# A two-layer hybrid trunk: ten of the 22 tiles of the third FFN by seven products, all hyena filters beside the first FFN, the modulations spread anew, one pool of five PSUM banks

## The chip, the cores and the metric

The kernel runs on one core of a Trainium2 chip. The metric is the time of one execution on the device in microseconds (us); lower is better. TensorE (PE in the profile) multiplies matrices, VectorE (DVE) and ScalarE (ACT) work elementwise, GpSimd (POOL) takes a few small operations, SyncE (SP) issues the DMAs. Each engine works through its own instructions in the order of the program and waits on semaphores.

## The reference

Two layers act on 640 tokens of width 1024: 128 context tokens and 512 latent tokens. Each layer is an FFN, a group of four token mixers, and a second FFN, each behind a normalization that is scaled and shifted by a modulation of the layer:

```python
mod = (jax.nn.silu(cond) @ lp['w_mod'] + lp['b_mod'])[:, None, :]
sh1, sc1, g1, sh2, sc2, g2, sh3, sc3, g3 = jnp.split(mod, N_MOD, axis=-1)
x = x + 0.5 * g1 * swiglu(modulate(rmsnorm(x, nw[0]), sh1, sc1), lp['ffn_w_in'][0], lp['ffn_w_out'][0])
y, s_ssd, s_ret, k, v = token_mixing(modulate(rmsnorm(x, nw[1]), sh2, sc2), lp, ssd_s0, ret_s0, ctx_kv)
x = x + g2 * y
x = x + 0.5 * g3 * swiglu(modulate(rmsnorm(x, nw[2]), sh3, sc3), lp['ffn_w_in'][1], lp['ffn_w_out'][1])

def swiglu(h, w_in, w_out):
    gate, up = jnp.split(h @ w_in, 2, axis=-1)
    return (jax.nn.silu(gate) * up) @ w_out
```

The inner width of an FFN is 2816, 22 tiles of 128. One of the mixers is hyena: a long convolution whose kernels ("filters") come from a small network with sines that depends on the weights alone, not on the tokens.

## The kernel before

The work on the tokens is a chain of stages, with `x` kept transposed in SBUF as 8 tiles of 128 features by 640 tokens, in two halves g = 0 and 1 of 320 columns: FFN1, mixers and FFN2 of layer 0, then FFN3, mixers and FFN4 of layer 1. A scheduler orders the instructions of each engine when the program is built; at run time the order is fixed.

**Products.** Every fp32 operand is split into a high and a low part (`hi`, `lo` of a weight; `hh`, `hl` of the normalized x; `gh`, `gl` of the gated product). The high part is a ScalarE cast, the low part a VectorE subtraction (`split`, `wsplit`). A product is then three matmuls (`mm3`): hi by hh, hi by hl, lo by hh. TensorE can't take the third one before VectorE has written `lo`.

**FFN1 and FFN3** use `ffn`: 22 direct tiles, each with a gate and an up weight of 1024 columns, 2 weights x 2 halves x 8 x 3 = 96 matmuls. The shift of the modulation rides as two more columns in half 0 (322 columns). After each chunk of tiles (5, 5, 5, 4, 3) a down pass multiplies by the output weights and adds into `x` (`accumulate`, the `x<-mm,gate,x` rows).

**FFN2 and FFN4** use `ffn7`: two direct tiles (320 columns), then 20 "quads". A quad computes the 2x2 block product of one tile's gate and up weights with the two halves by seven products instead of eight: 7 x 4 x 3 = 84 matmuls. VectorE adds weight blocks into `sa` and `sb` and splits them; the sums of the token blocks (`nv<-nv`, split into `th` and `tl`) are formed once at the start of the stage, by `sums`, behind each of the first two direct tiles. The first product of a quad goes into a PSUM tile `mb`, the second into `mm`, the third (`T3`, which needs `sa`) into `mc`. `norm7` is the normalization that leaves the sums' raw material behind; `norm` is that of `ffn`.

**Modulations.** Except for a few at the start, each 128-row tile of `w_mod` is loaded by DMA (`wm`) and reduced on VectorE against the broadcast condition, once for each of two conditions (`wmj<-wm,condb`, a "piece", pinned in the order of the program), then a small addition writes `mod`. A generator yields piece by piece; `ffn` and `ffn7` take them at a rate (RATES) per half-tile, per column of a down pass or per quad, from a list (`todo`) for each FFN.

**Filters.** The filters of layer 0 stand beside FFN1, those of layer 1 beside FFN3: small matmuls, sines, and DMAs to DRAM.

Of the kernel before, what the change touches and what calls it, by code (L numbers as in the profile page):

```python
# [19 lines left out]
EPS = 1e-6  # L20
NEG = -1.0e30
GCOLS = ((0, 128, 0), (128, 320, 1)), ((0, 320, 1),)
FFN_CHUNKS = (5, 5, 5, 4, 3), (4, 4, 4, 4, 3, 3)
KMAIN = 19


# [27 lines left out]
class Trunk:  # L54
# [38 lines left out]
        self.nc.tensor.transpose(out, in_, self.ident[b : b + n, b : b + n])  # L93

    def mx(self, *shape):

        self.turn = (self.turn + 1) % 5
        if self.wide and self.turn >= 3:
            t = self.xtp.tile([128, 512], F32, tag="xt", name="mx")
        else:  # L100
            t = self.mxp.tile([128, 512], F32, tag="mx", name="mx")
        return self.shaped(t, shape)

    @staticmethod
# [23 lines left out]
    def setup(self):  # L128
        tc, nc, ctx, I = self.tc, self.nc, self.ctx, self.I
        pool = lambda name, bufs=1, **k: ctx.enter_context(tc.tile_pool(name=name, bufs=bufs, **k))  # L130
        self.cp = cp = pool("const")
        self.sp = pool("small", 2)
        self.wp = pool("w", 3)
        self.ringp = pool("ring", NB)
        self.mmp = pool("mmp", 3, space=PSUM)
        self.xtp = pool("xtp", 2, space=PSUM)
        self.mxp = pool("mxp", 3, space=PSUM)
        self.turn, self.wide = 0, True
        self.ssum, self.V = {}, {}
# [283 lines left out]
    def ffn(self, li, w, todo, rate, after_group, ahead=()):  # L423
        I, n = self.I, 2 * w
        ff = 0
        with self.tc.tile_pool(name="ffn", bufs=2, side="right", reuse_waits="tile") as mp, self.tmp(), \
                self.tc.tile_pool(name="mods", bufs=1, side="right", reuse_waits="tile") as modp:
            mods = self.modulation(todo, modp, bufs=MBUF, pin=PIN) if todo else iter(())
            credit = 0.0
            for ci, nk in enumerate(FFN_CHUNKS[0]):  # L430
                G = []
                for f in range(ff, ff + nk):
                    wg, wu = (ahead[i] if 2 * f + i < len(ahead) else self.wload(I["ffnin"][li, w, 2 * f + i], 1024)
# [22 lines left out]
                            next(mods, None)  # L456
                            credit -= 1.0
                    G.append([(gh[:, 320 * g : 320 * g + 320], gl[:, 320 * g : 320 * g + 320]) for g in range(2)])
                if ci == len(FFN_CHUNKS[0]) - 1:
                    for _ in mods:  # L460
                        pass
                if ci < len(FFN_CHUNKS[0]) - 1:
                    for m in range(8):
                        hi, lo = self.wload(I["ffnoutA"][li, w, m, :, ff * 128 : (ff + nk) * 128], nk * 128)
                        for g in range(2):
# [27 lines left out]
    def quad(self, li, w, f, sp, mp, halves):  # L493
# [12 lines left out]
        add(sa[:, 1], sb[:, 0], a11, SUB)  # L506
        add(sb[:, 1], a12, sa[:, 1], SUB)
        new = lambda pool, tag, name: pool.tile([128, 512], F32, tag=tag, name=name)[:, :320]
        A, B, C = new(self.mmp, "mm", "mm"), new(self.xtp, "xt", "mb"), new(self.xtp, "xt", "mc")
        sg = mp.tile([128, 640], F32, tag="sg", name="sg", bufs=2)  # L510

        def copied(ps, name):
# [32 lines left out]
        self.split(gh[:, o:], gl[:, o:], sg[:, o:])  # L545
        self.G.append([(gh[:, 320 * g : 320 * g + 320], gl[:, 320 * g : 320 * g + 320]) for g in range(2)])

    def ffn7(self, li, w, todo, rate, after_group):
        I, n = self.I, 2 * w
        pool = lambda name: self.tc.tile_pool(name=name, bufs=2, side="right", reuse_waits="tile")  # L550
        with pool("ws") as sp, pool("ffn") as mp, pool("mods") as modp, self.tmp():
            self.wide = False
            mods = self.modulation(todo, modp, bufs=MBUF, pin=PIN) if todo else iter(())
            credit = 0.0
            self.G = []

            def finish(q):
                for _ in q:
# [2 lines left out]
            def down(ff, nk):  # L561

                G, self.G = self.G[:nk], self.G[nk:]
                for m in range(8):
                    hi, lo = self.wload(I["ffnoutA"][li, w, m, :, ff * 128 : (ff + nk) * 128], nk * 128)
                    for g in range(2):
                        ps = self.mmp.tile([128, 512], F32, tag="mm", name="mm")[:, :320]
                        self.mm3(ps, [(hi[:, k * 128 : (k + 1) * 128], lo[:, k * 128 : (k + 1) * 128]) + G[k][g]
                                      for k in range(nk)])
                        self.accumulate(li, n, m, g, ps)  # L570
                    next(mods, None)

            def direct(f):

# [4 lines left out]
                for g in range(2):  # L579
                    c = slice(320 * g, 320 * g + 320)  # L580
                    self.act(sg[:, c], self.unit(ws[0], g, shifts=False), AF.Silu)
                    self.tt(sg[:, c], self.unit(ws[1], g, shifts=False), sg[:, c], MUL)
                    self.split(gh[:, c], gl[:, c], sg[:, c])
                self.G.append([(gh[:, 320 * g : 320 * g + 320], gl[:, 320 * g : 320 * g + 320]) for g in range(2)])

            for f in range(NDIR):
                direct(f)
                if f < 2:
                    self.sums(f)
            for j in range(2):  # L590
                self.split(self.hw[0][1][:, 2 * j : 2 * j + 2, 0:320], self.hw[1][1][:, 2 * j : 2 * j + 2, 0:320], self.V[0][j])
            ends = [sum(FFN_CHUNKS[1][: i + 1]) for i in range(len(FFN_CHUNKS[1]))]
            prev = None
            for f in range(NDIR, 22):
                q = self.quad(li, w, f, sp, mp, f == 21)
                next(q)
                if prev is not None:
                    next(prev)
                next(q)
                if prev is not None:  # L600
                    finish(prev)
                    if f in ends:
                        ci = ends.index(f)
                        down(f - FFN_CHUNKS[1][ci], FFN_CHUNKS[1][ci])
                prev = q
                credit += rate
                while credit >= 1.0:
                    next(mods, None)
                    credit -= 1.0
            finish(prev)  # L610
            for _ in mods:
                pass
            nk = FFN_CHUNKS[1][-1]
            ws = [self.wload(I["ffnoutB"][li, w, b], 1024) for b in range(3)]
            G = self.G
            for g in range(2):
                for m in range(8):
# [7 lines left out]
                                      ws[b][1][:, j * 128 : (j + 1) * 128]) + G[k][g])  # L625
                    self.mm3(ps, parts)
                    self.accumulate(li, n, m, g, ps)
                    if li + 1 < NL:
                        self.square(m, g)
                if g:  # L630
                    next(done, None)
                done = after_group(g)
                next(done, None)
            next(done, None)
            self.wide = True


    def sin(self, pool, a, ps, b, fr):
# [684 lines left out]

    def mixers(self, li, kern):
        I = self.I
        if FPOS[li] == 2:
            kern.update(self.filters([li]))
        hy = [[self.conv_unit(li, 2 * j + h, PC.hy_cw, PC.hy_cb, 2 * j + h, False) for h in range(2)] for j in range(3)]
        if FPOS[li] == 3:
            kern.update(self.filters([li]))  # L1330
        YH = self.hyena(li, hy, *kern[li])
        Y = list(YH)
        for name in ORDER:
# [83 lines left out]
    def run(self):  # L1417
        self.setup()
        with self.tc.tile_pool(name="start", bufs=2, side="right", reuse_waits="tile") as p, self.tmp():
# [16 lines left out]
            ahead = [self.wload(self.I["ffnin"][0, 0, i], 1024) for i in range(2)]  # L1436
            for n in norms:
                next(n, None)
        kern = self.filters([0]) if FPOS[0] == 0 else {}
        todo = [[(0, i) for i in range(2, 9)] + [(1, 0)], [(1, 1)],  # L1440
                [(1, i) for i in range(2, 9)], []]
        for li in range(NL):
            def n1(g):
                if g == 0:
# [47 lines left out]
EACT = 1
# [164 lines left out]
```

## Time and profile before

| | |
|---|---|
| median of 3 runs | 2803.92 us (2802.38 to 2805.83) |
| profiled execution | 2796.57 us |
| its span in the profile | 2794.8 us |
| mean granted TensorE clock | 0.987 of full speed |
| PE, DVE, ACT busy | 97%, 69%, 36% |
| DMA | 300.52 MB, mean 108 GB/s |

The profile shows one execution. Busy shares are averages over stages that have different limits; which engine is waited for is read from single stretches. In this kernel the FFNs lie at about 56 to 563 us, 985 to 1410, 1437 to 1932 and 2354 to 2795, the mixers at 565 to 960 and 1946 to 2332, with short transitions between them.

### The profile page before, as it was taken

Reading aid. Unit: us, or ns where it says so; the run is one execution under the profiler, and the core shown is the slowest. Engines: PE = TensorE matmul, PEld = TensorE weight load, DVE = VectorE, ACT = ScalarE, POOL = GpSimd, SP = SyncE. Lnnn points to the kernel's source line nnn. Section 1 sums busy time; section 2 is a strip of 40 time slices with the busy share of each in tenths; the row PEclk is TensorE's granted clock in tenths of the full one; section 3 lists DMA queues with packets and bytes.
Section 4 is the critical chain, followed back from the end, with each engine's and each line's share of the span. In section 5 each row is a group of like instructions: output and inputs, shape, how many; then the busy total and the mean of one; then the engine's idle time right before and its main releaser. Section 6 shows DMA issues by size and latency. Waiting matters only on the chain.

```text
span 2794.8 us, 45752 instructions
## 1 busy us (share of the span) xinstructions
PE 2708.9 (97%) x17990; PEld 2601.4 (93%) x17990; DVE 1921.8 (69%) x4040; ACT 1001.2 (36%) x2047; POOL 115.6 (4%) x191
## 2 busy tenths in 40 slices
PE   5999999999999999999999999999999999999999
PEld 3899999999889899999989999998999888999999
DVE  5867677666765688766677676676568467766666
ACT  3222222332544353333442223223336434334432
POOL 0000000100010200000020000002001002000000
PEclk9999999999999999999999999999999999999999
DMA  7454544421213123222235444443213021222222
GB/s 265 145 183 144 159 143 162 136 81 63 80 51 99 52 76 117 85 86 76 82 138 181 146 144 137 143 155 99 80 57 101 18 72 59 83 81 72 83 73 94
DMA packets 121169, 300.52 MB, mean 108 GB/s; under 512 B 20062, under 2 KB 44974, under 8 KB 120572
## 3 DMA queue, kind: packets, MB, share of 16 engines
q1 hardware_dynamic: 120956, 297.61, 33.1%
q8 instruction: 142, 2.33, 0.3%
q14 instruction: 71, 0.58, 0.1%
HBM read 283.36 MB, written 14.20 MB: 106 GB/s over the span
## 4 chain that ended last, share of the span: by engine, by line
PE 89%; DVE 5%; POOL 1%; issue 1%; ACT 1%; DMA 1%; SPq 0%; POOLq 0%; ACTq 0%; DVEq 0%
PE mm L88 70%; PE mx L88 10%; PE mc L88 5%; PE mb L88 3%; PE mx L93 2%; DVE lo L61 1%; DVE x L70 1%; POOL nsum L294 1%; ACT hi L76 0%; DMA E<-cumd 0%; DVE wmj L278 0%; DVE hl L61 0%; DVE nx L70 0%; DVE gl L61 0%; POOL nrs L125 0%
## 5 line engine op out<-in xcount | busy, mean ns | idle before, releaser
L88 PE MATMUL mm<-hh,hi 128*128 128x320 f32 (+2 forms) x3136 | 993.0, 317 | 9.1 <-ACT hh L76 4.0
L88 PE MATMUL mm<-hh,lo 128*128 128x320 f32 (+2 forms) x3136 | 989.5, 316 | 7.7 <-DVE lo L61 7.7
L88 PE MATMUL mm<-hl,hi 128*128 128x320 f32 (+2 forms) x3136 | 990.4, 316 | 2.1 <-DVE hl L61 2.1
L76 ACT CAST hi<-raw 128x1024 fp32r<-128x1024 f32 (+4 forms) x406 | 346.0, 852 | 858.1 <-PE mm L88 809.4
L88 PEld LDWEIGHTS mm<-hh,hi 128*128 128x128 f32 (+1 forms) x3136 | 596.6, 190 | 19.3 <-ACT hh L76 5.6
L88 PEld LDWEIGHTS mm<-hh,lo 128*128 128x128 f32 (+1 forms) x3136 | 598.9, 191 | 16.0 <-DVE lo L61 8.4
L88 PEld LDWEIGHTS mm<-hl,hi 128*128 128x128 f32 (+1 forms) x3136 | 597.1, 190 | 13.5 <-issue 5.6
L61 DVE TENSOR_TENSOR lo<-raw,hi 128x1024 fp32r<-128x1024 f32 (+4 forms) x406 | 395.5, 974 | 183.0 <-ACT hi L76 182.0
L88 PE MATMUL mm<-gh,hi 128*128 128x320 f32 x1408 | 437.5, 311 | 7.2 <-DVE x L70 6.7
L88 PE MATMUL mm<-gl,hi 128*128 128x320 f32 x1408 | 435.2, 309 | 1.8 <-DVE gl L61 1.4
L88 PE MATMUL mm<-gh,lo 128*128 128x320 f32 x1408 | 434.5, 309 | 0.0
L70 DVE SCALAR_TENSOR_TENSOR x<-mm,gate,x 128x128 f32<-128x128 f32 (+2 forms) x624 | 253.8, 434 | 181.1 <-PE mm L88 178.6
L278 DVE CUSTOM_DVE_ANT_0 wmj<-wm,condb 128x1024 bf16<-128x1024 f32 x264 | 321.2, 1217 | 2.4 <-ACT condb L73 1.2
L88 PEld LDWEIGHTS mm<-gh,hi 128*128 128x128 f32 x1408 | 264.3, 188 | 13.6 <-PE mm L88 9.7
L88 PEld LDWEIGHTS mm<-gl,hi 128*128 128x128 f32 x1408 | 264.4, 188 | 5.8 <-DVE gl L61 4.4
L88 PEld LDWEIGHTS mm<-gh,lo 128*128 128x128 f32 x1408 | 264.5, 188 | 0.0
L70 DVE SCALAR_TENSOR_TENSOR gu<-mm,cg,sg 128x128 f32<-128x128 f32 x132 | 54.2, 436 | 157.7 <-ACT cg L76 103.6
L294 POOL TENSOR_TENSOR nsum<-nsum,nsq 128x320 f32<-128x320 f32 x60 | 54.2, 904 | 1384.3 <-ACT nsq L73 946.6
L88 PE MATMUL mc<-th,lo 128*128 128x320 f32 x320 | 98.7, 309 | 0.1
L88 PE MATMUL mc<-th,hi 128*128 128x320 f32 x320 | 98.7, 308 | 0.0
L88 PE MATMUL mc<-tl,hi 128*128 128x320 f32 x320 | 98.6, 308 | 0.0
L76 ACT COPY cg<-mm 128x2 f32<-128x2 f32 x88 | 14.1, 160 | 213.6 <-PE mm L88 213.2
(283 smaller groups left out, 3247.6 us busy)
## 6 DMA issues: line engine op xcount, KB each, us to landing
raw<-in_ffnin SPq DMA_DIRECT2D x176, 512.0 KB, 3.5
wm<-in_wmodT SPq DMA_DIRECT2D x132, 512.0 KB, 3.6
raw<-in_mixin SPq DMA_DIRECT2D x52, 512.0 KB, 3.4
raw<-in_ffnoutA SPq DMA_DIRECT2D x80, 256.0 KB, 2.6
raw<-in_ffnoutA SPq DMA_DIRECT2D x48, 320.0 KB, 2.8
wms<-in_wmod SPq DMA_DIRECT2D x12, 512.0 KB, 3.4
raw<-in_ffnoutB SPq DMA_DIRECT2D x12, 512.0 KB, 3.4
raw<-in_mixout SPq DMA_DIRECT2D x16, 384.0 KB, 3.0
```

The source lines that it names most:

```text
L61: self.nc.vector.tensor_tensor(out, a, b, op=op)
L70: self.nc.vector.scalar_tensor_tensor(out, a, s, b, op0=op0, op1=op1)
L76: self.nc.scalar.copy(out, in_)
L88: return self.nc.tensor.matmul(out, lhsT=lhsT, rhs=rhs, start=start, stop=stop, **k)
L93: self.nc.tensor.transpose(out, in_, self.ident[b : b + n, b : b + n])
L278: return self.nc.vector.tensor_tensor_reduce(junk, raw, cb, 1.0, 0.0, op0=MUL, op1=ADD, accum_out=out)
L294: (adder or (self.nc.vector if g and m > 5 else self.nc.gpsimd)).tensor_tensor(s, s, sq, op=ADD)
```

## The change

- FFN3 moves from `ffn` to `ffn7`, with 12 direct tiles and 10 quads; FFN2 and FFN4 keep 2 and 20. The transition into FFN3 therefore uses `norm7`.
- All FFNs use the chunks 5, 5, 5, 4, 3; `ffn7` now runs down passes among the direct tiles too.
- The filters of both layers are computed beside FFN1.
- The modulations are divided among the FFNs in another way, FFN4 gets some, and `ffn7` takes them at three rates: per direct half-tile, per column of a down pass, per quad.
- The two PSUM pools of 2 and 3 banks become one of 5.

```diff
-FFN_CHUNKS = (5, 5, 5, 4, 3), (4, 4, 4, 4, 3, 3)
+FFN_CHUNKS = 5, 5, 5, 4, 3
...
-        self.turn = (self.turn + 1) % 5
-        if self.wide and self.turn >= 3:
-            t = self.xtp.tile([128, 512], F32, tag="xt", name="mx")
-        else:
-            t = self.mxp.tile([128, 512], F32, tag="mx", name="mx")
+        t = self.mxp.tile([128, 512], F32, tag="mx", name="mx")
...
-        self.xtp = pool("xtp", 2, space=PSUM)
-        self.mxp = pool("mxp", 3, space=PSUM)
-        self.turn, self.wide = 0, True
+        self.mxp = pool("mxp", 5, space=PSUM)
...
-        A, B, C = new(self.mmp, "mm", "mm"), new(self.xtp, "xt", "mb"), new(self.xtp, "xt", "mc")
+        A, B, C = new(self.mmp, "mm", "mm"), new(self.mxp, "mx", "mb"), new(self.mxp, "mx", "mc")
...
-    def ffn7(self, li, w, todo, rate, after_group):
+    def ffn7(self, li, w, todo, ndir, rates, after_group):
...
-            credit = 0.0
             self.G = []
+            credit = [0.0]
+
+            def some(rate):
+
+                credit[0] += rate
+                while credit[0] >= 1.0:
+                    next(mods, None)
+                    credit[0] -= 1.0
...
-                    next(mods, None)
+                    some(rates[1])
...
                     self.split(gh[:, c], gl[:, c], sg[:, c])
+                    some(rates[0])
...
-            for f in range(NDIR):
+            ends = [sum(FFN_CHUNKS[: i + 1]) for i in range(len(FFN_CHUNKS))]
+            for f in range(ndir):
                 direct(f)
                 if f < 2:
                     self.sums(f)
+                if f + 1 in ends:
+                    nk = FFN_CHUNKS[ends.index(f + 1)]
+                    down(f + 1 - nk, nk)
...
                 prev = q
-                credit += rate
-                while credit >= 1.0:
-                    next(mods, None)
-                    credit -= 1.0
+                some(rates[2])
...
-        kern = self.filters([0]) if FPOS[0] == 0 else {}
-        todo = [[(0, i) for i in range(2, 9)] + [(1, 0)], [(1, 1)],
-                [(1, i) for i in range(2, 9)], []]
+        kern = self.filters(range(NL))
+        todo = [[(0, i) for i in range(2, 9)], [(1, 0), (1, 1)],
+                [(1, i) for i in range(2, 8)], [(1, 8)]]
...
-                    if g == 0:
-                        self.shifts(li + 1, 0)
-                    yield from self.norm(li + 1, 0, g)
+                    yield from self.norm7(li + 1, 0, g)
...
-            self.ffn(li, 0, todo[2 * li], RATES[2 * li], n1, () if li else ahead)
+            if li == 0:
+                self.ffn(li, 0, todo[0], RATES[0], n1, ahead)
+            else:
+                self.ffn7(li, 0, todo[2], NDIR[1], RATES[2], n1)
+                self.fac.close()
...
-            self.ffn7(li, 1, todo[2 * li + 1], RATES[2 * li + 1], n3)
-            self.fac.close()
+            self.ffn7(li, 1, todo[2 * li + 1], NDIR[2 * li], RATES[2 * li + 1], n3)
+        self.fac.close()
...
-NDIR = 2
+NDIR = 2, 12, 2
...
-RATES = 2.3, 1.0, 1.9, 1.0
+RATES = 2.0, (1.5, 1.0, 0.5), (2.2, 1.0, 1.0), (2.0, 1.0, 3.0)
```

**How it moves instructions.** VectorE before, in the second direct tile of FFN2 and the first quad, up to the split of that quad's first sum (`lo<-sa`); the split of the quad's gate weights, `lo<-raw` 128x1024, stands five rows ahead of these, and the first modulation piece of the stage comes eleven rows behind them:

```order
L61 TENSOR_TENSOR tl<-nv,th 128x2x320
L61 TENSOR_TENSOR gl<-sg,gh 128x320
L61 TENSOR_TENSOR nv<-nv 128x640
L61 TENSOR_TENSOR sb<-raw 128x512
L61 TENSOR_TENSOR sa<-sb,raw 128x512
L61 TENSOR_TENSOR tl<-nv,th 128x2x320
L61 TENSOR_TENSOR hl_109<-nv,hh_107 128x640
L61 TENSOR_TENSOR sg<-mm,sg 128x320
L61 TENSOR_TENSOR hl_109<-nv,hh_107 128x640
L61 TENSOR_TENSOR gl<-sg,gh 128x320
L61 TENSOR_TENSOR sb<-raw,sa 128x512
L61 TENSOR_TENSOR lo<-sa,hi 128x1024
```

VectorE now, at the same place:

```order
L271 ISA wmj,mod_108<-wm,condb 128x1024
L271 ISA mod_108 128x1
L61 TENSOR_TENSOR hl_106<-nv,hh_104 128x640
L271 ISA wmj,mod_108<-wm,condb 128x1024
L271 ISA mod_108 128x1
L61 TENSOR_TENSOR lo<-raw,hi 128x1024
L61 TENSOR_TENSOR mod_108<-mod_108,par_93 128x2
L61 TENSOR_TENSOR sa<-raw 128x512
L61 TENSOR_TENSOR sb<-raw 128x512
L61 TENSOR_TENSOR sa<-sb,raw 128x512
L61 TENSOR_TENSOR sb<-raw,sa 128x512
L61 TENSOR_TENSOR lo<-sa,hi 128x1024
```

Six pieces stand between the first `sg<-mm` of FFN2 and this `lo<-sa`, two of them shown; the split of the gate weights and all four sums have moved behind the last. In FFN4 there are eight. TensorE at the first quad of FFN2 before, from the last direct matmul on:

```order
L88 MATMUL mm<-hh_107,lo 128x320
L88 MATMUL mb<-hh_106,hi 128x320
L88 MATMUL mb<-hl_108,hi 128x320
L88 MATMUL mb<-hh_106,lo 128x320
L88 MATMUL mb<-hh_106,hi 128x320
```

and now:

```order
L88 MATMUL mm<-hh_104,lo 128x320
L88 MATMUL mb<-hh_103,hi 128x320
L88 MATMUL mb<-hl_105,hi 128x320
L88 MATMUL mm<-hh_103,hi 128x320
L88 MATMUL mm<-hl_105,hi 128x320
L88 MATMUL mb<-hh_103,lo 128x320
L88 MATMUL mb<-hh_103,hi 128x320
```

Two `mm`, which need only the high part of the weights, have moved ahead of the first `mb` that reads `lo`. VectorE in FFN3 now, from the third modulation piece behind the stage's first `sg<-mm` to the split of the second direct tile's up weights:

```order
L271 ISA wmj,mod_108<-wm,condb 128x1024
L271 ISA mod_108 128x1
L61 TENSOR_TENSOR nv<-nv 128x640
L271 ISA wmj,mod_108<-wm,condb 128x1024
L271 ISA mod_108 128x1
L61 TENSOR_TENSOR tl<-nv,th 128x2x320
L61 TENSOR_TENSOR mod_108<-mod_108,par_93 128x2
L61 TENSOR_TENSOR nv<-nv 128x640
L61 TENSOR_TENSOR lo<-raw,hi 128x1024
```

Before, FFN3 had no such sums (`nv`, `tl`) at all.

## Rows read from the trace of the kernel before

**Rows 1.** The page's part 1: busy time, share of the span, instructions
```profile
PE 2708.9 (97%) x17990; PEld 2601.4 (93%) x17990; DVE 1921.8 (69%) x4040; ACT 1001.2 (36%) x2047; POOL 115.6 (4%) x191
```

**Rows 2.** The chain of waits, pieces: start us, length us, what
```profile
1089.30 3.53 PE mm L88 x24
...
1509.40 409.44 PE mm L88 x2771
```

**Rows 3.** Waits of PE from 985 to 1400: total us, times, longest
```profile
PE mm L88 <- DVE x L70: 2.8, 5, 0.6
```

**Rows 4.** Busy us by stretch: length, PE, PEld, DVE, ACT, POOL, clock, DMA
```profile
58.00:130.00 72.00, 71.81 (x388) 61.74 (x387) 59.41 (x131) 21.39 (x43) 0.29 (x2) 0.98 0.52 165
987.62:1011.09 23.47, 23.47 (x159) 23.19 (x158) 22.77 (x35) 13.49 (x23) 0.00 (x0) 1.00 0.08 25
1018.50:1100.90 82.40, 81.53 (x547) 80.22 (x546) 69.02 (x129) 31.02 (x50) 0.00 (x0) 1.00 0.38 120
1432.00:1512.00 80.00, 79.76 (x434) 69.36 (x433) 66.08 (x145) 22.74 (x50) 0.29 (x2) 0.97 0.49 150
2359.87:2383.32 23.45, 23.45 (x159) 23.28 (x158) 22.77 (x35) 13.47 (x23) 0.00 (x0) 1.00 0.08 24
```

**Rows 5.** Timeline of DVE at the start of FFN2: start us, length us, instruction
```profile
987.62 0.48 DVE L61 TENSOR_TENSOR sg<-mm,sg 128x320 f32<-128x320 f32 x1
...
993.45 0.49 DVE L61 TENSOR_TENSOR sg<-mm,sg 128x320 f32<-128x320 f32 x1 [0.17 <-ACT sg L73]
993.86 0.82 DVE L61 TENSOR_TENSOR nv<-nv 128x640 f32<-128x640 f32 x1
994.59 0.82 DVE L61 TENSOR_TENSOR tl<-nv,th 128x640 fp32r<-128x640 f32 x1
...
999.07 1.21 DVE L61 TENSOR_TENSOR lo<-raw,hi 128x1024 fp32r<-128x1024 f32 x1
1000.21 0.81 DVE L61 TENSOR_TENSOR tl<-nv,th 128x640 fp32r<-128x640 f32 x1
...
1007.73 0.49 DVE L61 TENSOR_TENSOR sg<-mm,sg 128x320 f32<-128x320 f32 x1 [0.30 <-PE mm L88]
...
1009.87 1.22 DVE L61 TENSOR_TENSOR lo<-sa,hi 128x1024 fp32r<-128x1024 f32 x1
```

**Rows 6.** Timeline of PE at the start of FFN2
```profile
999.02 0.31 PE L88 MATMUL mm<-hh,lo 128*128 128x320 f32 x1
...
1007.84 0.31 PE L88 MATMUL mb<-hh,lo 128*128 128x320 f32 x1
...
1011.38 0.30 PE L88 MATMUL mc<-th,lo 128*128 128x320 f32 x1
```

**Rows 7.** Timeline of DVE at the start of FFN4
```profile
2382.10 1.22 DVE L61 TENSOR_TENSOR lo<-sa,hi 128x1024 fp32r<-128x1024 f32 x1
```

**Rows 8.** Timeline of PE at FFN4's first quad
```profile
2383.61 0.30 PE L88 MATMUL mc<-th,lo 128*128 128x320 f32 x1
```

**Rows 9.** The page's part 5, costliest groups: busy us, mean ns, idle before
```profile
L278 DVE CUSTOM_DVE_ANT_0 wmj<-wm,condb 128x1024 bf16<-128x1024 f32 x264 | 321.2, 1217 | 2.4 <-ACT condb L73 1.2
```

**Rows 10.** Timeline of DVE around one modulation piece in a quad of FFN2
```profile
1018.57 1.22 DVE L278 CUSTOM_DVE_ANT_0 wmj<-wm,condb 128x1024 bf16<-128x1024 f32 x1
1019.72 0.08 DVE L278 DVE_READ_ACCUMULATOR2_ANT mod<- 128x1 f32 x1
1019.72 1.22 DVE L61 TENSOR_TENSOR lo<-sb,hi 128x1024 fp32r<-128x1024 f32 x1
```

**Rows 11.** Busy time by stretch, as in rows 4, around two stops of PE
```profile
915.00:918.00 3.00, 1.25 (x10) 0.90 (x9) 2.61 (x12) 0.00 (x0) 1.01 (x1) 1.00 0.00 0
918.00:925.00 7.00, 6.08 (x23) 6.04 (x24) 4.65 (x13) 1.13 (x2) 1.01 (x1) 0.51 0.17 56
1423.00:1437.00 14.00, 9.79 (x43) 8.26 (x42) 11.10 (x22) 4.03 (x8) 3.42 (x3) 0.63 0.48 165
```

**Rows 12.** Waits of PE from 0 to 58: total us, times, longest
```profile
PE mx L88 <- ACT modrow L76: 2.6, 3, 1.5
```

More of the change, by code (lines that the diff above doesn't have):

```diff
@@ L429, in ffn @@
             credit = 0.0
-            for ci, nk in enumerate(FFN_CHUNKS[0]):
+            for ci, nk in enumerate(FFN_CHUNKS):
                 G = []
@@ L458, in ffn @@
                     G.append([(gh[:, 320 * g : 320 * g + 320], gl[:, 320 * g : 320 * g + 320]) for g in range(2)])
-                if ci == len(FFN_CHUNKS[0]) - 1:
+                if ci == len(FFN_CHUNKS) - 1:
                     for _ in mods:
                         pass
-                if ci < len(FFN_CHUNKS[0]) - 1:
+                if ci < len(FFN_CHUNKS) - 1:
                     for m in range(8):
@@ L551, in ffn7 @@
         with pool("ws") as sp, pool("ffn") as mp, pool("mods") as modp, self.tmp():
-            self.wide = False
             mods = self.modulation(todo, modp, bufs=MBUF, pin=PIN) if todo else iter(())
-            credit = 0.0
             self.G = []
+            credit = [0.0]
[4 more added lines that the diff above has]
+                    credit[0] -= 1.0
             def finish(q):
@@ L589, in ffn7 @@
                     self.sums(f)
+                if f + 1 in ends:
+                    nk = FFN_CHUNKS[ends.index(f + 1)]
+                    down(f + 1 - nk, nk)
             for j in range(2):
                 self.split(self.hw[0][1][:, 2 * j : 2 * j + 2, 0:320], self.hw[1][1][:, 2 * j : 2 * j + 2, 0:320], self.V[0][j])
-            ends = [sum(FFN_CHUNKS[1][: i + 1]) for i in range(len(FFN_CHUNKS[1]))]
             prev = None
-            for f in range(NDIR, 22):
+            for f in range(ndir, 22):
                 q = self.quad(li, w, f, sp, mp, f == 21)
@@ L603, in ffn7 @@
                         ci = ends.index(f)
-                        down(f - FFN_CHUNKS[1][ci], FFN_CHUNKS[1][ci])
+                        down(f - FFN_CHUNKS[ci], FFN_CHUNKS[ci])
                 prev = q
-                credit += rate
-                while credit >= 1.0:
-                    next(mods, None)
-                    credit -= 1.0
+                some(rates[2])
             finish(prev)
@@ L612, in ffn7 @@
                 pass
-            nk = FFN_CHUNKS[1][-1]
+            nk = FFN_CHUNKS[-1]
             ws = [self.wload(I["ffnoutB"][li, w, b], 1024) for b in range(3)]
@@ L627, in ffn7 @@
                     self.accumulate(li, n, m, g, ps)
-                    if li + 1 < NL:
+                    if li + 1 < NL or w == 0:
                         self.square(m, g)
@@ L634, in ffn7 @@
             next(done, None)
-            self.wide = True
     def sin(self, pool, a, ps, b, fr):
@@ L1325, in mixers @@
         I = self.I
-        if FPOS[li] == 2:
-            kern.update(self.filters([li]))
         hy = [[self.conv_unit(li, 2 * j + h, PC.hy_cw, PC.hy_cb, 2 * j + h, False) for h in range(2)] for j in range(3)]
-        if FPOS[li] == 3:
-            kern.update(self.filters([li]))
         YH = self.hyena(li, hy, *kern[li])
@@ L1459, in n3 @@
                     yield
-            if li and FPOS[1] == 0:
-                kern.update(self.filters([li]))
-            self.ffn(li, 0, todo[2 * li], RATES[2 * li], n1, () if li else ahead)
+            if li == 0:
[3 more added lines that the diff above has]
+                self.fac.close()
             for m in range(8):
@@ L1478 @@
 MPARTS = (0, 1, 2, 3, 4, 5), (6, 7)
-FPOS = (0, 0)
 ALAG = 2
```

## Prediction

> **What bounds the kernel now.** I read the page's busy shares first: TensorE is busy for 97% of the span, VectorE for 69% [rows 1]. A share over the whole span hides stages, so the chain of waits came next. Its longest piece is a bare run of 2771 matmuls in 409.44 us, 0.1478 us each, and in a quad 24 take 3.53 us, 0.147 us each [rows 2]. So in the FFNs a matmul that is removed is worth about 0.1475 us, as long as nothing else makes TensorE wait. In FFN2 hardly anything does: the worst kind of wait there, for the x update of VectorE, comes five times and sums to 2.8 us [rows 3].
>
> Then I asked which engine would be next, by busy time in single stretches [rows 4]. The steady quads of FFN2, one modulation piece to each, leave VectorE idle for 13.4 of 82.4 us. The first 23.5 us of FFN2 and of FFN4 are another matter: VectorE is busy for 22.77 of 23.47 and of 23.45 us. In these stretches it finishes the normalization (hl), forms the sums for the seven products (nv, tl), splits two weight tiles and prepares the first quad. The timeline shows how close that is. The stretch starts at T, the first `sg<-mm` (987.62), and ends with `lo<-sa`, which starts at 1009.87 and takes 1.22, so 1011.09 [rows 5]. TensorE's first matmul that reads this tile is `mc<-th,lo` at 1011.38 [rows 6]: a slack of 0.3 us. The VectorE idle time of the stretch is in three pieces of 0.20, 0.17 and 0.30 us, of which two are shown. FFN4 is a copy: `lo<-sa` ends at 2382.10 + 1.22 = 2383.32, `mc<-th,lo` starts at 2383.61 [rows 7, 8]. TensorE runs without a gap there only because nothing else is on VectorE.
>
> **The change part by part.** *Ten quads in FFN3.* A direct tile has 96 matmuls on the way up and a quad 84. Ten tiles change: 10 x 12 x 0.1475 = **-17.7 us**. In the other twelve tiles, the two columns of the shift leave the 320-column half: 1056 matmuls of 322 columns become 320; by columns that is 1056 x 2/320 x 0.1478 = **-0.9 us** (an estimate from the cadence of rows 2). The new chunks change how many down passes lie between quads: FFN2 and FFN4 have one fewer, FFN3 gains two. At 2.8/5 = 0.56 us of waiting for each [rows 3] that cancels; I take 0, bounds -3 and +3.
>
> *Modulations.* The number of pieces stays 264, at 1217 ns each [rows 9]; the next instruction starts 1.15 us after one [rows 10]. What changes is where they stand. In FFN2 and FFN4 they were absent from the two direct tiles. Now a direct half-tile asks for 1.5 and 2.0 of them, and the order of VectorE shows the result: between T and the first `lo<-sa` stand six pieces in FFN2 and eight in FFN4, with three and four small mod additions (0.07 us each, an estimate from the read behind a piece, 0.08 [rows 10]). All the old work of the stretch (four hl, eight nv, six tl, two weight splits, four additions) is still ahead of that `lo<-sa`. So VectorE has 6 x 1.15 + 3 x 0.07 = 7.1 us more to do in FFN2 before TensorE can go on, and 8 x 1.15 + 4 x 0.07 = 9.5 us in FFN4. The slack takes 0.3 and the idle pieces up to 0.67. That leaves 6.1 to 6.8 us, I take **+6.7**, and 8.5 to 9.2, I take **+9.0**: between ends this near, the upper part, because the third idle piece is a wait for TensorE itself, which is at the same place. Most of it shows at the third matmul of a quad's first product: `lo<-raw` of the gate weights, which before was split at 999.07 and wanted at 1007.84, now stands behind the last piece, and TensorE's new order has two `mm` between the second and the third `mb`. The rest shows at `mc<-th,lo`.
>
> [...] In the rows of before, too, VectorE goes through the stretch in the order of its program. [...]
>
> *The same in FFN3.* There the first two tiles are direct as well, at 2.2 pieces per half-tile. Four pieces stand ahead of the split of the second tile's up weights. Counting the starts of rows from the first `sg<-mm` of FFN3 with the steps of before (0.41 for 320 columns, 0.73 for 640, 1.14 for a weight split [rows 5], 1.15 for a piece), that split ends at T + 13.4. TensorE comes to it at about T + 11.4 (before, in FFN2: 999.02 - 987.62 [rows 5, 6]). **+2.0 us**, bounds 0 and 3. The ten quads that follow have one piece each, as those of FFN2 had, which ran with VectorE at 69.02 of 82.4 us and TensorE at 81.53 [rows 4]: nothing. Later direct tiles last 96 x 0.1478 = 14.2 us and hold four or five pieces, 5.8 us, beside some 4 us of splits: nothing.
>
> *The clock.* When TensorE stands still in this kernel, the granted clock falls afterwards. From 915 to 918 it is busy for 1.25 of 3.00 us, and the next 7 us are granted 0.51. From 1423 to 1437 it is busy for 9.79 of 14 and granted 0.63 on average [rows 11]. [...] What the clock takes is 7 x 0.49 = 3.4 us in the first case and at most 14 x 0.37 = 5.2 us in the second. Part of that hides the second wait (at half clock VectorE catches up), so I take 3.0 for each of the two long waits, **+6.0**, bounds 0 and +10. [...]
>
> *Filters of both layers beside FFN1.* TensorE is busy for 71.81 of 72 us beside those of layer 0, and 79.76 of 80 us beside those of layer 1 [rows 4]. VectorE has 59.41 and 66.08 us in them, so it covers them in either place: 0, bounds 0 and +3. *`norm7` at the end of FFN2* keeps the order of TensorE there (4 matmuls, 5 for the statistics, 8, 1), and the wait for the last adds remains: 0, bounds -5 (no fall of the clock there any more) and +2. *Start*: the sums that build the first modulations are now spread, 8 then 2, where 12 stood together; the wait for the copied row is 2.6 us in three today [rows 12]; I take **+0.5**, bounds -1 and +1.5. *One pool of five PSUM banks*: in quads `mb` and `mc` now share five banks instead of having two; in the mixers the total stays five. 0, bounds -2 and +3.
>
> Sum: -17.7 - 0.9 + 6.7 + 9.0 + 2.0 + 6.0 + 0.5 = +5.6. On the profiled execution, 2796.57 (span 2794.8, 1.8 around it), that is 2802.2. The median of the three runs is 2803.92, 7.35 above that execution, so the forecast is **2809.5 us**.
>
> **The rivals.** *B, waits without the clock.* Waits of 6.7 and 9.0 may not bring a half-clock stretch, since the shares of rows 11 are those of several gaps and of short work between them. Sum -0.4: 2803.5. For it: the fall at 915 comes after more than one gap. Against it: rows 11.
>
> *C, VectorE arrives ahead.* If at T VectorE has already done part of the hl, nv and tl that it does after T today, the pieces fall into that room. Then the three waits and the clock go: -18.1, **2785.8**. This is the case on the other side. It decides from the point at which the three waits and the clock together cost less than 12.5 us, since -18.1 + 12.5 = -5.6; that is a lead of about 5 us in FFN2 and in FFN4, which takes the clock's 6.0 with it. For it: VectorE idles 13 of 82 us in the quads, so on average there is room. Against it: its order after T holds the same four hl, eight nv and six tl as today.
>
> *D, the quads of FFN3 or the mixers wait as well.* If each new quad waits 1 us (for a sum that VectorE prepares behind a late piece), +10: 2819.6; the same mechanism can turn the saving of 17.7 to nothing at 1.77 us a quad, the case that the change doesn't do what it says. For it: the raw weights of the quads come through three buffers that VectorE empties. Against it: FFN2 runs just so today.
>
> **How the numbers follow.** A 0.2% difference is 5.6 us, about the least that a measurement of this kernel can tell from none: faster means below 2798.3, slower above 2809.5. The forecast stands on that border. Chances: the forecast 0.55 (its terms' bounds give 2803 to 2818; 0.24 of it under 2809.5, 0.31 above), B 0.17 (2800 to 2806, a sliver faster), C 0.17 (2784 to 2799), D 0.11 (2816 to 2830). So faster 0.17, same 0.41, slower 0.42. The forecast's own range is 2803 to 2818; with part of C and of D, 8 in 10 lie in 2795 to 2819.
>
> **What would show it.** In the profile after, FFN2 and FFN4 should each show one TensorE wait of 6 to 9 us for `lo` of VectorE at the first `mb`, with VectorE fully busy before it and `wmj` rows ahead of that `lo`; then a granted clock near 0.5 for several us. FFN3 from its first quad to its last should take 12 x 0.1475 = 1.8 us less per tile than a direct one. The steady quads should show no wait on VectorE beyond what rows 3 show. The forecast is wrong if TensorE passes the first quads without a gap (C), or if gaps turn up at every quad of FFN3 (D), or in FFN1, where the second layer's filters now stand.

## The result and the profile after

The changed kernel takes 2775.69 us in the median (2773.57 to 2785.97, 4 runs), the kernel before 2803.15 beside it: a ratio of 0.9911, interval 0.9887 to 0.9936. It is faster by 27 us. The forecast was 2809.5, its range 2795 to 2819; the result lies below that, and below the 2784 to 2799 of rival C as well. The profiled execution took 2773.57, its span is 2771.8.

The page of the changed kernel, the line that answers to [rows 1]:

```profile
span 2771.8 us, 45385 instructions
PE 2671.7 (96%) x17870; PEld 2575.6 (93%) x17870; DVE 1959.7 (71%) x4050; ACT 1030.2 (37%) x2042; POOL 114.0 (4%) x191
```

TensorE has 120 matmuls fewer, as it should, but 37 us less of busy time, twice what 120 matmuls cost. So the traces are cut into stages, at the last matmul ahead of a normalization's statistics: those of the second half behind an FFN, those of the first half behind the mixers. The table has the lengths in us; "to mixers" is the start and FFN1 together. The first two lines are the two kernels, the others the experiments below. A line is one profiled execution, which can be off the kernel's median (e2's is 5.6 us below it, e5b's 5.3 above):

| kernel | to mixers | mixers 0 | FFN2 | FFN3 | mixers 1 | FFN4 | span |
|---|---|---|---|---|---|---|---|
| before | 558.6 | 401.5 | 463.4 | 509.2 | 399.7 | 462.5 | 2794.8 |
| changed | 591.1 | 384.3 | 466.9 | 476.5 | 383.7 | 469.3 | 2771.8 |
| e1_two_pools | 588.2 | 392.2 | 470.5 | 476.1 | 399.9 | 468.7 | 2795.7 |
| e2_one_pool | 562.9 | 382.9 | 463.1 | 513.3 | 382.0 | 462.0 | 2766.3 |
| e3_no_pieces_first | 591.4 | 383.2 | 462.9 | 471.5 | 384.4 | 458.7 | 2752.0 |
| e4_filters_split | 563.3 | 384.4 | 468.3 | 535.3 | 382.4 | 468.4 | 2802.0 |
| e5b_old_chunks | 593.3 | 383.7 | 465.4 | 472.0 | 385.7 | 464.9 | 2765.1 |
| e6_17_quads | 594.3 | 382.9 | 460.1 | 477.9 | 384.5 | 460.6 | 2760.2 |
| e7_filters_only | 587.8 | 391.9 | 466.9 | 481.5 | 400.8 | 462.4 | 2791.3 |
| e8_four_banks | 590.2 | 385.5 | 471.9 | 476.3 | 385.7 | 472.9 | 2782.7 |
| e9_pieces_spread | 593.2 | 384.2 | 462.5 | 468.2 | 383.9 | 458.0 | 2750.1 |
| e10_all_direct | 593.5 | 383.7 | 462.7 | 483.3 | 384.1 | 461.3 | 2768.6 |
| e11_13_quads | 594.1 | 384.4 | 462.3 | 469.7 | 385.0 | 458.4 | 2753.9 |

FFN1 has taken over filters from FFN3 and is 32.5 us longer with the start; FFN3, which also has the quads and a wait, is 32.7 us shorter. The waits that were forecast are there: FFN4 is longer. What the forecast didn't have is in the mixers, 17.2 and 16.0 us shorter, with the same work. First the waits. TensorE at the first quads of FFN2 and FFN4 and in the second tile of FFN3, changed kernel, timeline (start, length, idle before and who ended it):

```profile
1022.84 0.31 PE L88 MATMUL mm<-hl,hi 128*128 128x320 f32 x1
1029.16 0.64 PE L88 MATMUL mb<-hh,lo 128*128 128x320 f32 x1 [6.01 <-DVE lo L61]
1029.59 0.47 PE L88 MATMUL mb<-hh,hi 128*128 128x320 f32 x1
1029.86 0.47 PE L88 MATMUL mb<-hl,hi 128*128 128x320 f32 x1
...
1032.21 0.31 PE L88 MATMUL mm<-hh,hi 128*128 128x320 f32 x1
1032.36 0.31 PE L88 MATMUL mm<-hl,hi 128*128 128x320 f32 x1
...
1463.97 0.30 PE L88 MATMUL mm<-hl,hi 128*128 128x320 f32 x1
1471.05 0.64 PE L88 MATMUL mm<-hh,lo 128*128 128x320 f32 x1 [6.78 <-DVE lo L61]
...
2350.32 0.31 PE L88 MATMUL mm<-hl,hi 128*128 128x320 f32 x1
2359.01 0.63 PE L88 MATMUL mb<-hh,lo 128*128 128x320 f32 x1 [8.39 <-DVE lo L61]
```

VectorE ahead of the first of them, the rows that answer to [rows 5]:

```profile
1002.63 0.48 DVE L61 TENSOR_TENSOR sg<-mm,sg 128x320 f32<-128x320 f32 x1
...
1024.86 1.22 DVE L271 CUSTOM_DVE_ANT_0 wmj<-wm,condb 128x1024 bf16<-128x1024 f32 x1
...
1026.74 1.21 DVE L271 CUSTOM_DVE_ANT_0 wmj<-wm,condb 128x1024 bf16<-128x1024 f32 x1
...
1027.89 1.22 DVE L61 TENSOR_TENSOR lo<-raw,hi 128x1024 fp32r<-128x1024 f32 x1
```

The split that TensorE wants stands right behind the last piece and ends at 1029.11, TensorE goes on at 1029.16. Busy time and clock around the three waits (columns as in [rows 4]):

```profile
1024.00:1032.00 8.00, 2.84 (x11) 2.84 (x12) 7.76 (x13) 0.86 (x1) 0.00 (x0) 0.58 0.20 66
1468.00:1476.00 8.00, 4.95 (x19) 4.95 (x20) 7.97 (x12) 1.21 (x2) 0.00 (x0) 0.57 0.56 191
2356.00:2364.00 8.00, 4.99 (x21) 4.99 (x22) 7.38 (x10) 1.88 (x3) 0.00 (x0) 0.54 0.32 110
```

The granted clock is 0.54 to 0.58 over 8 us each time, partly while TensorE still waits. Now the mixers. Both stages of the kernel before, then of the changed one:

```profile
558.55:960.07 401.52, 386.34 (x2640) 361.26 (x2638) 254.79 (x676) 164.32 (x424) 25.41 (x59) 0.98 0.23 74
1932.64:2332.30 399.66, 389.60 (x2639) 363.72 (x2638) 253.86 (x675) 163.00 (x422) 25.82 (x59) 0.97 0.22 69
```

```profile
591.11:975.40 384.29, 374.89 (x2640) 355.93 (x2638) 254.18 (x676) 166.75 (x425) 24.67 (x59) 0.99 0.24 77
1918.79:2302.46 383.67, 374.94 (x2639) 356.08 (x2638) 254.23 (x676) 165.32 (x423) 24.78 (x59) 0.99 0.25 84
```

The counts of TensorE are equal, 2640 and 2639 matmuls; the order is not. In the kernel before, two stops in layer 0 look like this:

```profile
758.94 0.66 PE L88 MATMUL mx<-u,E 128*128 128x64 f32 x4 [2.37 <-DVE E L61]
...
764.27 0.53 PE L88 MATMUL mm<-hh,lo 128*128 128x322 f32 x1 [1.91 <-DVE lo L61]
764.60 0.47 PE L88 MATMUL mm<-hh,hi 128*128 128x322 f32 x1
```

TensorE waits for one chain of the mixers with no matmul of another one behind it in its order, and then runs at 0.27 us a matmul (764.60 to 764.87), granted 0.50 for 3.4 us. Summed over both stages, idle time falls from 25.2 to 18.1 us (lengths less busy time), and what the clock takes, by granted clock in stretches of 4 us, from 20.5 to 10.2 us. The rest, some 16 us, is in closer starts of the matmuls. Fewer changes between `mx` matmuls and `mm` ones (344 before, 316 now) go with that; that they are its cause is not shown.

The changed kernel loses no clock between the transitions: behind a mixer stage's first normalization it is granted 0.50 for 10.2 us (from 595.2 and from 1923.0), and from there to the stage's end 1.00.

```profile
605.50:975.40 369.90, 364.66 (x2599) 347.25 (x2597) 243.19 (x654) 160.45 (x414) 20.71 (x39) 1.00 0.23 76
1933.30:2302.46 369.16, 364.63 (x2598) 347.32 (x2597) 243.10 (x654) 160.51 (x414) 20.69 (x39) 1.00 0.24 78
```

So its 10.2 us lie at the transitions. The kernel before has four falls in between, which take about 12 of its 20.5 us: 3.4 us long at 764.4, 6.9 at 918.0, 6.8 at 2266.3 and 2290.2. The one at 2266.3 has no stop ahead of it; TensorE is busy throughout, the last 4 us with small `mx` matmuls alone:

```profile
2240.00:2254.00 14.00, 13.98 (x105) 13.03 (x105) 10.21 (x30) 10.87 (x36) 0.00 (x0) 1.00 0.65 203
2254.00:2266.30 12.30, 12.30 (x107) 10.92 (x107) 8.18 (x29) 4.28 (x12) 0.00 (x0) 1.00 0.30 92
2266.30:2273.10 6.80, 6.80 (x30) 5.77 (x29) 2.64 (x9) 0.00 (x0) 1.01 (x1) 0.50 0.01 2
```

### The profile page after: what moved, and what is told of

It is laid out like the page before. It is cut to its first block, busy times and chain, and to the rows that moved or that the text cites. A ratio compares the mean times of both kernels' runs of the same rounds, so it can differ in the third digit from the quotient of the medians.

```text
span 2771.8 us, 45385 instructions
## 1 busy us (share of the span) xinstructions
PE 2671.7 (96%) x17870; PEld 2575.6 (93%) x17870; DVE 1959.7 (71%) x4050; ACT 1030.2 (37%) x2042; POOL 114.0 (4%) x191
## 4 chain that ended last, share of the span: by engine, by line
PE 89%; DVE 5%; issue 2%; POOL 1%; ACT 1%; DMA 1%; SPq 0%; POOLq 0%; DVEq 0%; ACTq 0%
PE mm L88 68%; PE mx L88 10%; PE mc L88 6%; PE mb L88 3%; PE mx L93 2%; DVE lo L61 1%; POOL nsum L287 1%; DVE x L70 1%; DVE wmj L271 1%; ACT hi L76 0%; POOL nrs L120 0%; DVE hl L61 0%; DVE tl L61 0%; DVE nv L61 0%; DVE gl L61 0%
## 5 line engine op out<-in xcount | busy, mean ns | idle before, releaser
L88 PE MATMUL mm<-hh,lo 128*128 128x320 f32 (+2 forms) x2936 | 922.8, 315 | 13.0 <-DVE lo L61 13.0
L88 PE MATMUL mm<-hh,hi 128*128 128x320 f32 (+2 forms) x2936 | 927.6, 317 | 6.8 <-ACT hh L76 4.1
L88 PE MATMUL mm<-hl,hi 128*128 128x320 f32 (+2 forms) x2936 | 924.3, 315 | 2.5 <-DVE hl L61 2.1
L76 ACT CAST hi<-raw 128x1024 fp32r<-128x1024 f32 (+3 forms) x390 | 338.5, 868 | 779.0 <-PE mm L88 704.4
L88 PEld LDWEIGHTS mm<-hh,lo 128*128 128x128 f32 (+1 forms) x2936 | 558.8, 190 | 20.3 <-DVE lo L61 14.1
L88 PEld LDWEIGHTS mm<-hh,hi 128*128 128x128 f32 (+1 forms) x2936 | 557.1, 190 | 15.0 <-ACT hh L76 5.7
L88 PEld LDWEIGHTS mm<-hl,hi 128*128 128x128 f32 (+1 forms) x2936 | 556.9, 190 | 12.8 <-issue 5.1
L61 DVE TENSOR_TENSOR lo<-raw,hi 128x1024 fp32r<-128x1024 f32 (+3 forms) x390 | 387.6, 994 | 175.0 <-ACT hi L76 172.9
L76 ACT CAST gh<-sg 128x640 fp32r<-128x640 f32 (+1 forms) x85 | 51.6, 607 | 103.7 <-DVE sg L61 103.7
L70 DVE SCALAR_TENSOR_TENSOR gu<-mm,cg,sg 128x128 f32<-128x128 f32 (+2 forms) x66 | 27.2, 435 | 76.2 <-ACT cg L76 49.0
```

The costliest lines, as they stand in the source:

```text
L61: self.nc.vector.tensor_tensor(out, a, b, op=op)
L70: self.nc.vector.scalar_tensor_tensor(out, a, s, b, op0=op0, op1=op1)
L76: self.nc.scalar.copy(out, in_)
L88: return self.nc.tensor.matmul(out, lhsT=lhsT, rhs=rhs, start=start, stop=stop, **k)
```

## The experiments

Each changes only what its diff shows (`...` stands for unchanged lines, and for lines that a sentence names); times are medians, ratios are against the kernel before, with their interval.

**Is it the pool?** e1 is the changed kernel with the two old pools, e2 the kernel before with the new one. e2's diff (e1's is its reverse on the changed kernel):

```diff
-        self.turn = (self.turn + 1) % 5
-        if self.wide and self.turn >= 3:
-            t = self.xtp.tile([128, 512], F32, tag="xt", name="mx")
-        else:
-            t = self.mxp.tile([128, 512], F32, tag="mx", name="mx")
+        t = self.mxp.tile([128, 512], F32, tag="mx", name="mx")
...
-        self.xtp = pool("xtp", 2, space=PSUM)
-        self.mxp = pool("mxp", 3, space=PSUM)
-        self.turn, self.wide = 0, True
+        self.mxp = pool("mxp", 5, space=PSUM)
...
-        A, B, C = new(self.mmp, "mm", "mm"), new(self.xtp, "xt", "mb"), new(self.xtp, "xt", "mc")
+        A, B, C = new(self.mmp, "mm", "mm"), new(self.mxp, "mx", "mb"), new(self.mxp, "mx", "mc")
...
-            self.wide = False
...
-            self.wide = True
```

> The changed kernel with the two PSUM pools of before (2 banks for mb and mc and for two of five general tiles, 3 banks for the rest). All else as changed. Theory P (the single pool sped up the mixers, through another order of TensorE's work in them): the two mixer stages, 384 and 384 us in the changed kernel, go back to about 400 each, and the time rises by 33 us from 2775.7 to about 2807, a little above the kernel before. Rival M (the mixers are faster because the filters, the modulations or the seven-product stage behind them moved, not because of the pool): the mixers stay at 384, time 2773 to 2779. Rival S (TensorE's order differs by chance with every change of the program): mixers anywhere between, no clear 33 us.

2797.83 us, 0.9984 (0.9974 to 0.9993): 22 us of the 27 are gone. The mixers take 392.2 and 399.9 us.

> The kernel before with only the single pool of five banks. Theory P: mixers fall from 401.5 and 399.7 us to about 384 each, time 2803 - 33 = about 2770, and TensorE passes the first quads of FFN2 and FFN4 with no wait. Rival M: mixers stay near 400, time 2800 to 2806. Under P the rest of the change together is worth 2775.7 - 2770 = +5 us, close to what was forecast for it.

2773.69 us, 0.9896 (0.9879 to 0.9912). The mixers take 382.9 and 382.0 us:

```profile
562.89:945.83 382.94, 374.76 (x2639) 355.72 (x2638) 254.39 (x676) 167.15 (x426) 24.56 (x59) 0.99 0.25 78
1922.22:2304.25 382.03, 372.90 (x2639) 353.45 (x2638) 254.34 (x675) 165.33 (x424) 25.15 (x59) 1.00 0.23 72
```

The pool alone gives 29 us, as much as the whole change within the intervals; M is out. In layer 0, TensorE's order between the two transitions is that of the changed kernel, run for run of like matmuls. S is half right: with two pools the order of layer 0 differs from program to program (401.5, 391.9 and 392.2 us; the last two share one order). By the code, a counter hands out the turns of the two pools, and everything ahead of the mixers uses it up. In layer 1 the three programs with two pools have one order and take 399.7 to 400.8 us. With one pool, none of the 20 mixer stages in the table takes more than 385.7 us. Whether two pools with another start of the counter would come as low was not tried.

**Five banks, or any free bank?** e8 is the changed kernel with a pool of four banks.

```diff
-        self.mxp = pool("mxp", 5, space=PSUM)
+        self.mxp = pool("mxp", 4, space=PSUM)
```

> The changed kernel with a single pool of four PSUM banks instead of five; one bank stays unused. Theory F (what helps the mixers is that a tile may take any bank that is free, where in two pools it was bound beforehand to one of them): with a bank fewer the mixers still take at most 390 us each, below the 400 of two pools with five banks, time 2776 to 2788. Rival N (five free banks are what counts): mixers 395 us and more, time 2800 or above.

2783.47 us, 0.9926 (0.9911 to 0.9941); mixers 385.5 and 385.7, so four banks that anyone may take serve them better than two and three. F holds against N; that a free bank is the reason was not tested in another way. The time lost against five banks is in FFN2 and FFN4, 5.0 and 3.6 us, and there in the clock: over these stages the granted clock takes 11.9 and 12.6 us, where it took 5.1 and 8.5 in the changed kernel (3.4 and 5.1 of that around the waits). That the fifth bank decides this isn't shown.

**The waits.** e3 takes the pieces out of the first two tiles of each seven-product FFN:

```diff
-                    some(rates[0])
+                    some(rates[0] if f >= 2 else 0.0)
...
-                [(1, i) for i in range(2, 8)], [(1, 8)]]
+                [(1, i) for i in range(2, 9)], []]
...
-RATES = 2.0, (1.5, 1.0, 0.5), (2.2, 1.0, 1.0), (2.0, 1.0, 3.0)
+RATES = 2.0, (0.0, 1.0, 1.0), (3.2, 1.0, 1.0), (0.0, 0.0, 0.0)
```

> The changed kernel, in which the first two direct tiles of each seven-product FFN take no modulation pieces: FFN2 takes 1 per quad and per column, FFN3 3.2 per half-tile from its third tile on and the last modulation of layer 1 as well, FFN4 none. The number of pieces is the same. Theory W (the waits of 6.0 at FFN2, 6.8 at FFN3 and 8.4 us at FFN4 are the pieces ahead of the weight split, and each brings 3 to 4 us at half clock): all three go, -21 us of waiting and about -10 of clock, time 2745 to 2752. Rival C (the wait only moves: VectorE falls behind later by the same work): at most -8, time 2768 to 2776.

2754.26 us, 0.9827 (0.9813 to 0.9842), 21 us below the changed kernel; the three waits are gone. It is less than W said: FFN2, FFN3 and FFN4 got 4.0, 5.0 and 10.6 us shorter. In FFN2 the clock gave nothing back, since a new fall of 6.8 us at its end (from 1424.3, granted 0.50) takes the place of the one at the wait. For FFN3, TensorE's waits from 1870 to 1900 show why:

```profile
PE mm L88 <- DVE x L70: 4.4, 4, 1.8
```

3.2 per half-tile don't finish the list of 112 pieces (64 + 32 + 10 = 106), and the last six come in a lump. e9 takes 3.6:

```diff
-RATES = 2.0, (0.0, 1.0, 1.0), (3.2, 1.0, 1.0), (0.0, 0.0, 0.0)
+RATES = 2.0, (0.0, 1.0, 1.0), (3.6, 1.0, 1.0), (0.0, 0.0, 0.0)
```

> As the run without pieces in the first tiles (2754.3), but FFN3 takes 3.6 pieces per half-tile instead of 3.2, so that its list is done before the last chunk. Theory (the two gaps of 2.1 us near the end of FFN3 there are pieces left over, issued in one lump): both gaps go, 2750. Rival: the gaps are something else and stay, 2754.

2752.14 us, 0.9816 (0.9802 to 0.9830). Both gaps went and FFN3 is 3.3 us shorter. One wait is new, 2.7 us at the third product of the second quad. The medians of the two versions stand beside different runs of the kernel before, so 2 us between them is not measured.

**The quads.** e10 is e9 with all tiles of FFN3 direct; the two conditions only let the stage end without a quad:

```diff
-                if f + 1 in ends:
+                if f + 1 in ends[:-1]:
...
-            finish(prev)
+            if prev is not None:
+                finish(prev)
...
-NDIR = 2, 12, 2
+NDIR = 2, 22, 2
...
-RATES = 2.0, (0.0, 1.0, 1.0), (3.6, 1.0, 1.0), (0.0, 0.0, 0.0)
+RATES = 2.0, (0.0, 1.0, 1.0), (3.0, 1.0, 1.0), (0.0, 0.0, 0.0)
```

> As the run with the pieces spread (about 2750), but FFN3 with 22 direct tiles and no quad, pieces at 3.0 per half-tile from its third tile on. Theory (ten quads are worth ten times 12 matmuls, 17.7 us, the first term of the forecast): FFN3 longer by 16 to 20 us, time 2766 to 2770. Rival (the saving of the quads is lost in waits within them): less than 10 us, time below 2760.

2768.5 us, 0.9873 (0.9858 to 0.9887), 16.4 above e9 beside the same runs of the kernel before, and FFN3 is 15.1 us longer: the theory holds, a little under its 16 to 20. More of them: e6 has 17 quads (its diff is against e3), e11 13 (against e9).

```diff
-NDIR = 2, 12, 2
+NDIR = 2, 5, 2
...
-RATES = 2.0, (0.0, 1.0, 1.0), (3.2, 1.0, 1.0), (0.0, 0.0, 0.0)
+RATES = 2.0, (0.0, 1.0, 1.0), (3.2, 2.0, 2.0), (0.0, 0.0, 0.0)
```

> As the run without pieces in the first tiles (2754.3), but FFN3 with 5 direct tiles and 17 quads; the pieces at 3.2 per half-tile from the third tile on, 2 per column, 2 per quad. Theory (a quad is worth 12 matmuls, 1.77 us, as long as VectorE keeps up): 7 x 1.77 = 12.4 us less, 2742. Rival D (two pieces and a quad's 9.3 us of VectorE fill its 12.4 us, so TensorE waits in them): waits of 0.5 to 2 us a quad, no gain or a loss, 2750 to 2775.

2761.5 us, 0.9849 (0.9835 to 0.9864), 7 above e3. Its waits from 1480 to 1900, the first two of eight:

```profile
PE mc L88 <- DVE lo L61: 4.3, 3, 2.3
PE mc L88 <- ACT hi L76: 4.1, 2, 3.1
```

That is D: TensorE waits at the third product of quads for a late sum. e11:

```diff
-NDIR = 2, 12, 2
+NDIR = 2, 9, 2
...
-RATES = 2.0, (0.0, 1.0, 1.0), (3.6, 1.0, 1.0), (0.0, 0.0, 0.0)
+RATES = 2.0, (0.0, 1.0, 1.0), (3.6, 1.5, 1.2), (0.0, 0.0, 0.0)
```

> As the run with the pieces spread, but FFN3 with 9 direct tiles and 13 quads, pieces at 3.6 per half-tile, 1.5 per column, 1.2 per quad. Theory (VectorE still covers it): 3 x 1.77 = 5.3 us less, about 2745. Rival (waits at quads as in the run with 17 of them): 2750 to 2757.

2751.91 us, 0.9814 (0.9798 to 0.9830): no different from e9. The rival's time came, but not its waits: the profiled execution, 3.9 us above the median, has a single wait at the third product of a quad, 1.5 us in the second one. Where the 5.3 us went stays open. e9 and e11 are the fastest versions here, 53 us below the kernel before.

**The filters.** e7 is the kernel before with both layers' filters beside FFN1, e4 the changed kernel with those of layer 1 beside FFN3.

```diff
-        kern = self.filters([0]) if FPOS[0] == 0 else {}
+        kern = self.filters(range(NL))
...
-            if li and FPOS[1] == 0:
-                kern.update(self.filters([li]))
```

> The kernel before with only the filters of layer 1 moved beside FFN1; two PSUM pools, FFN3 all direct tiles. Theory (their place is free beside direct tiles): FFN1 longer by about 28 us, FFN3 shorter by as much, time 2803 within 4 us apart from the first mixer stage, whose order may differ because the filters use up turns of the two pools: it came out at 401.5 us before and 392 us with two pools and the filters moved. So 2794 to 2804. Rival (the place by itself gives the 28 us that it was worth beside seven products): 2770 to 2780.

2791.59 us, 0.9950 (0.9933 to 0.9967). FFN1 +29.2, FFN3 -27.7: the place is free. The profiled gain is in mixers 0, -9.6, where the order is that of e1; what was expected for that stage came.

> The changed kernel with the filters of layer 1 back beside the start of FFN3, the rest as changed. Theory (their place is worth nothing, TensorE does the same matmuls): FFN1 shorter by 29 to 33 us, FFN3 longer by as much, time 2775.7 within 4 us. Rival (beside seven products and pieces VectorE can't cover them): FFN3 longer by 35 to 45 us and new waits at its start, time 2780 to 2790.

2804.07 us, 1.0006 (0.9997 to 1.0016). Here the place is not free: FFN1 is 27.8 us shorter and FFN3 58.8 longer, more than even the rival said. It is lost at the start of the stage, long before its first quad. Waits of TensorE from 1416 to 1500:

```profile
PE mx L88 <- issue: 13.3, 2, 10.0
PE mx L88 <- ACT h L73: 7.3, 2, 4.8
PE mx L88 <- DVE pm L61: 3.2, 2, 1.6
```

TensorE waits in the filters' own chain, and its granted clock is 0.70 from 1430 to 1500. VectorE is busy for 46.95 of these 70 us, so it is not full, as the rival had it. Why "issue" takes 10 us in one piece there, this trace doesn't show.

**The chunks.** e5b is e3 with the old chunks in FFN2 and FFN4; `chunks` then stands for `FFN_CHUNKS` throughout `ffn7`:

```diff
+        chunks = (4, 4, 4, 4, 3, 3) if w else FFN_CHUNKS
...
```

> As the run without pieces in the first tiles (2754.3), but FFN2 and FFN4 again in six chunks of 4, 4, 4, 4, 3, 3 tiles. Theory (a chunk of four makes TensorE wait 0.7 us and more at the start of its down pass for the x update, a chunk of five doesn't, and there is one pass more): each of FFN2 and FFN4 longer by 4 us, time 2762. Rival (the chunks cancel, as the forecast had it): 2752 to 2757.

2761.59 us, 0.9854 (0.9840 to 0.9869): 7 us above e3. In the profiled executions FFN2 is 2.5 us longer, though the clock takes 3.4 less there, and FFN4 is 6.2 longer, of which the clock takes 3.7. The chunks don't cancel.

## Why the prediction was wrong

**One pool of five PSUM banks: 0, bounds -2 and +3.** This is the step that failed. It was costed by the number of banks, "in the mixers the total stays five", and so put at nothing. What decides is how the banks are bound to the tiles when the order is made. By e1 and e2 it is worth -22 to -29 us, by the mixers' stages -33. I had compared orders at the FFNs and the transitions, not in the mixers. There TensorE's order shows 329 runs of like matmuls in each layer (the same tile from the same inputs, the three matmuls of a product counted as like) instead of 372 and 353. That the single pool brings the better order, with four banks too, is shown (e2, e8); through which single tiles, not.

**Ten quads, -17.7:** right, 16.4 in e10. **Shift columns, -0.9:** 1056 matmuls are those of all 22 tiles; the twelve tiles that the term names have 576, which makes -0.5. No run tests it.

**Waits of 6.7, 9.0 and 2.0:** 6.0, 8.4 and 6.8 in the page's sense. In FFN2 and FFN4 the term was right to the place and the row. It rests on VectorE's order, and the trace shows that kept: the twelve rows printed for the changed kernel come one after the other, from 1024.86 (`wmj`) to 1032.21 (`lo<-sa`). The rest that was expected at `mc<-th,lo` was hidden in the half clock, as written: TensorE's matmuls start 0.27 us apart up to 1031.99, `lo<-sa` ends at 1033.44, and the matmul that reads it starts at 1033.85 without a wait. In FFN3 it was mis-sized by 5 us. VectorE there:

```profile
1454.76 0.82 DVE L61 TENSOR_TENSOR hl<-nv,hh 128x640 fp32r<-128x640 f32 x1 [2.58 <-ACT hh L76]
...
1457.15 0.48 DVE L61 TENSOR_TENSOR sg<-mm,sg 128x320 f32<-128x320 f32 x1
...
1469.78 1.22 DVE L61 TENSOR_TENSOR lo<-raw,hi 128x1024 fp32r<-128x1024 f32 x1
```

The split ended at T + 13.85 with T = 1457.15, near the T + 13.4 that I had counted. But T was no mark of TensorE: that `sg<-mm` stood behind late VectorE work and has no idle time before it. TensorE came to the split at 1464.12 (0.15 behind the start of its last matmul ahead of it, 1463.97), T + 7.0 and not T + 11.4.

**Clock, +6.0:** the three stretches above lie at 0.54 to 0.58 for 8 us, 3.4 to 3.7 us each, so there were three falls and not two, and some of the half clock runs while TensorE waits anyway. Waits and clock together were worth 21 us by e3 and 24 by e9, against 23.7 in the forecast. How much the clock takes in the same stages differs between kernels (e8), so 6.0 was no firm figure. Nor did every stop bring a fall: between the transitions of the changed kernel's mixer stages, stops of up to 1.8 us left the clock at 1.00. **`norm7`, 0:** the fall of the clock at the end of FFN2, which its bound of -5 let go, stayed: 6.8 us at 0.50 from 1445.1, where it was 10.2 us from 1426.6.

**Down passes, 0:** mis-sized, -7 by e5b. I counted the same wait at the x update [rows 3] for every pass and let the passes cancel. The waits are smaller in chunks of five; from 1050 to 1400 of the changed kernel they are 1.4 us, half of the 2.8 before, which explains a part of the 7:

```profile
PE mm L88 <- DVE x L70: 1.4, 4, 0.6
```

**Filters, 0:** right as costed (e7: +1.5). That leaving them at the start of a seven-product FFN3 would cost 28 (e4) was not asked. **Start, +0.5:** TensorE's first FFN1 matmul comes at 59.5 us instead of 55.8, +3.7, beyond the bound of +1.5. The pool alone brings this too: it comes at 59.4 in e2, and at 57.9 in e1.

**The rivals.** The time fell on the side of C, but not by C: the waits came. D came true only with more quads (e6). Without the pool the change is worth 2775.69 - 2773.69 = +2 us on top of e2, which is not clear of noise. e1, with a better turn in mixers 0 (-9.3), stands 5 us below the kernel before: 4 above without that. This is near the +5.6 of the sum, but in part by luck, as errors of opposite sign (the wait in FFN3 and the start against the chunks) cancel.

## What to carry to other kernels

When a change touches a pool or a counter that many stages share, compare the order of the longest stage that uses it, even where the diff seems to leave it alone; two pools filled by a fixed turn are not one pool of the same size (22 to 29 us apart here). Count VectorE's work in front of the instruction that TensorE waits for, but take the time at which TensorE arrives from TensorE's own rows. Work that may run at any time (the modulations) is best kept out of the few microseconds in which an engine is already full: that was worth 21 us more here.

## What the runs showed of the hardware

With TensorE at rest for 6.0 us, the clock fell while it was still waiting: behind the wait a matmul follows the other by 0.27 us (1029.59 to 1029.86), and by 0.15 us again from 1032.21 on. From 1024 to 1028, with no matmul, it was granted 0.66, from 1028 to 1032 0.50; the stretches of 8 us around the three waits have 0.54 to 0.58. The mixers of the kernel before show more than that. Their stops are at most 2.4 us each, and yet the two stages lose almost as much to the clock as to the stops themselves (20.5 and 25.2 us). And the fall at 2266.3 follows upon 26.28 busy of 26.30 us, so here the clock fell without TensorE having been idle; what brought it about this trace doesn't show. The same 2640 and 2639 matmuls in the order of the single pool had no fall between the transitions.
